# Cross-entropy over 32,000 classes on one core: label load on another ring, three buffers, short first loads, shrinking last loads, one table set

## The chip, the cores and the metric

The kernel runs on one core of a Trainium2 chip. The metric is the device time of one execution in microseconds (us). A profiled execution gives a span a little shorter than that time (2438.7 us against 2440.3 for the kernel before); details below are read from the span.

## The reference

```python
# logits: (16, 512, 32000) float32; labels: (16, 512) int32
logits_max = np.max(logits, axis=-1, keepdims=True)
log_sum_exp = np.log(np.sum(np.exp(logits - logits_max), axis=-1)) + logits_max.squeeze(-1)
log_probs = logits - log_sum_exp[..., np.newaxis]
loss = -log_probs[np.arange(batch)[:, None], np.arange(seq), labels]
```

There are 8192 rows of 32,000 values, 1048.6 MB, and each value is read once. Both kernels compute log(sum(exp(x))) minus the label's logit, without the maximum; for normally distributed logits that is safe.

## The kernel before

The 8192 rows lie on 128 partitions with 64 rows (row groups) each. A load brings 16,000 columns of one row group for all partitions, so each partition receives one contiguous piece of 64,000 bytes. ScalarE takes Exp in place and sums along the columns in the same instruction. The last three groups use loads of 4000 columns and five smaller buffers. The label logits are fetched by 64 gathers, one for each row group, issued from GpSimd.

```python
data_pool = ctx.enter_context(tc.tile_pool(name="data", bufs=2))
fine_pool = ctx.enter_context(tc.tile_pool(name="fine", bufs=5))
# ... cut ...
nc.sync.dma_start(out=labs64[:], in_=labels_pg)
# ... cut: iota and add on GpSimd make the gather's indices ...
for g in range(G):
    nc.gpsimd.indirect_dma_start(out=lab_logit[:, g:g + 1], ...)
# ... cut ...
for g in range(G):
    if g >= G - FINE_GROUPS:
        for c in range(CF):                       # 8 loads of 4000 columns
            tf = fine_pool.tile([P, WF], FP32)
            nc.sync.dma_start(out=tf[:], in_=lg_pg[:, g, c * WF:(c + 1) * WF])
            nc.scalar.activation(out=tf[:], in_=tf[:], func=Exp, accum_out=stats_col(g, c))
    else:
        for c in range(C):                        # 2 loads of 16000 columns
            t = data_pool.tile([P, W], FP32)
            nc.sync.dma_start(out=t[:], in_=lg_pg[:, g, c * W:(c + 1) * W])
            nc.scalar.activation(out=t[:], in_=t[:], func=Exp, accum_out=stats_col(g, c))

def finalize(lo, hi):
    nc.vector.reduce_sum(out=totals[:, lo:hi], ...)
    nc.scalar.activation(out=logsum[:, lo:hi], in_=totals[:, lo:hi], func=Ln)
    nc.vector.tensor_tensor(out=res[:, lo:hi], in0=logsum, in1=lab_logit, op=subtract)
    nc.scalar.dma_start(out=out_pg[:, lo:hi], in_=res[:, lo:hi])
finalize(0, G - 1)
finalize(G - 1, G)
```

## Time and profile before

| | before |
|---|---|
| median of 3 runs | 2440.26 us |
| span of the profiled run | 2438.7 us |
| ScalarE busy | 1754.4 us (72%) |
| start of the last Exp | 2430.84 us |
| from there to the end (the tail) | 7.9 us |

The first thing to ask is which engine has no time left. The following lines are from the windows view of the kernel before: the stretch in us, its length, the busy time of VectorE, ScalarE and GpSimd, the TensorE clock, the mean busy share of the 16 DMA engines, and what they moved.

```profile
core 0: us, DVE busy (x) ACT busy (x) POOL busy (x), PEclk, DMA share, GB/s
2.00:250.00 248.00, 0.00 (x0) 164.83 (x25) 60.38 (x65) 1.00 1.01 426
320.00:700.00 380.00, 0.00 (x0) 274.36 (x41) 0.00 (x0) 1.00 1.00 433
700.00:2290.00 1590.00, 0.00 (x0) 1145.91 (x169) 0.00 (x0) 1.00 1.00 433
```

The DMA engines are always busy and move 433 GB/s. The first stretch is slower, at 426 GB/s, and GpSimd is busy only there: it is issuing the gathers. ScalarE works in 66% of the first stretch and in 72% of the other two, so it waits for loads and not the reverse.

Two groups from the page of the kernel before say the same from ScalarE's side: instruction, shapes and count, then busy time and mean ns of one, then its idle time and what ended it.

```profile
L85 ACT ACTIVATE t<-t 128x16000 f32<-128x16000 f32 x122 | 1651.4, 13536 | 642.9 <-DMA t<-in_logits_dram 642.9
L76 ACT ACTIVATE tf<-tf 128x4000 f32<-128x4000 f32 x24 | 84.7, 3530 | 14.6 <-DMA tf<-in_logits_dram 14.6
```

An Exp of 16,000 columns takes 13.5 us, and ScalarE idles 642.9/122 = 5.3 us before each. As a buffer is loaded again as soon as its Exp ends, those 5.3 us are also what the *other* load still has to run when the new one is queued. That is why two buffers keep the queue filled.

The head, from the timeline of the kernel before (start, length, engine; SPq is SyncE's sequencer issuing DMAs; in brackets the idle time before and what ended it):

```profile
0.74 0.38 SPq L48 DMA_DIRECT2D labs<-in_labels_dram  x1
1.18 132.93 SPq L84 DMA_DIRECT2D t<-in_logits_dram  x8
2.79 0.32 POOL L53 TENSOR_TENSOR idx<-idx,labs 128x64 int32<-128x64 int32 x1 [1.78 <-DMA labs<-in_labels_dram]
24.64 13.54 ACT L85 ACTIVATE t<-t 128x16000 f32<-128x16000 f32 x1
```

The labels go first, and the logits wait 0.44 us for SyncE to issue them. The tail, from the same timeline:

```profile
2430.84 3.54 ACT L76 ACTIVATE tf<-tf 128x4000 f32<-128x4000 f32 x1 [1.11 <-DMA tf<-in_logits_dram]
2434.28 0.19 ACT L76 ACTIVATION_READ_ACCUMULATOR tf<-tf 128x1 f32 x1
2434.49 1.28 ACT L101 ACT_TABLE_LOAD   x1
2434.50 0.16 DVE L96 TENSOR_REDUCE totals<-stats_last 128x1 f32<-128x8 f32 x1 [36.37 <-ACT tf L76]
2435.78 0.20 ACT L101 ACTIVATE logsum<-totals 128x1 f32<-128x1 f32 x1
2436.02 0.16 DVE L105 TENSOR_TENSOR res<-logsum,lab_logit 128x1 f32<-128x1 f32 x1 [1.35 <-ACT logsum L101]
2436.21 0.34 ACTq L109 DMA_DIRECT2D out_dram<-res  x1
```

After the last load has landed, nothing overlaps the work that remains: an Exp over 4000 columns, a table load because Ln is not in the set that Exp had loaded, Ln, a subtraction, and a store of about 2.5 us until the span ends.

### The profile page before, as it was taken

What the parts mean: (1) busy time and instruction counts of PE and PEld (TensorE: products, weight loads), DVE (VectorE), ACT (ScalarE), POOL (GpSimd) and SP (SyncE); (2) the same over time, 40 slices, a digit from 0 to 9 for tenths busy, and PEclk for the clock granted to TensorE, in tenths of its full rate; (3) what the DMA queues carried; (4) which work ended last, traced back from release to release, by engine and by line L of the source; (5) the groups of instructions that cost most, each with busy time, mean ns of one, the idle gap of its engine ahead of it and who ended that gap; (6) DMA issues with size and microseconds to landing.
All of it is one profiled execution on the core that took longest, in us unless ns stands there. A gap on an engine that the chain in (4) does not pass through costs nothing.

```text
span 2438.7 us, 851 instructions
## 1 busy us (share of the span) xinstructions
DVE 1.7 (0%) x5; ACT 1754.4 (72%) x298; POOL 61.2 (3%) x70
## 2 busy tenths in 40 slices
DVE  0000000000000000000000000000000000000000
ACT  4777766777677767777677767777677767777697
POOL 3222000000000000000000000000000000000000
DMA  9999999999999999999999999999999999999998
GB/s 404 437 420 422 435 437 435 429 429 437 437 436 428 431 435 437 435 432 428 435 436 436 435 427 434 436 437 435 427 432 436 437 435 425 434 437 432 426 430 360
DMA packets 23510, 1048.77 MB, mean 430 GB/s; under 512 B 4688, under 2 KB 4816, under 8 KB 4816
## 3 DMA queue, kind: packets, MB, share of 16 engines
q1 hardware_dynamic: 21168, 1048.65, 99.6%
q0 software_dynamic: 2048, 0.04, 0.1%
q10 hardware_dynamic: 288, 0.03, 0.0%
q14 instruction: 6, 0.05, 0.0%
HBM read 1048.67 MB, written 0.03 MB: 430 GB/s over the span
## 4 chain that ended last, share of the span: by engine, by line
DMA 63%; ACT 36%; issue 0%; ACTq 0%; SPq 0%; DVE 0%
DMA t<-in_logits_dram 61%; ACT t L85 34%; DMA tf<-in_logits_dram 2%; ACT tf L76 2%; ACT L101 0%; ACT L76 0%; ACTq L85 0%; ACT logsum L101 0%; SPq L84 0%; DVE res L105 0%; SPq L48 0%; ACTq L109 0%; ACTq L76 0%
## 5 line engine op out<-in xcount | busy, mean ns | idle before, releaser
L85 ACT ACTIVATE t<-t 128x16000 f32<-128x16000 f32 x122 | 1651.4, 13536 | 642.9 <-DMA t<-in_logits_dram 642.9
L76 ACT ACTIVATE tf<-tf 128x4000 f32<-128x4000 f32 x24 | 84.7, 3530 | 14.6 <-DMA tf<-in_logits_dram 14.6
L57 POOL DMA_INDIRECT lab_logit<-in_logits_dram,idx x64 | 60.5, 945 | 186.8 <-DMA lab_logit<-in_logits_dram,idx 184.2
L85 ACT ACTIVATION_READ_ACCUMULATOR t<-t 128x1 f32 x122 | 22.7, 186 | 0.0
L85 ACT ACT_TABLE_LOAD x1 | 1.3, 1283 | 23.3 <-DMA t<-in_logits_dram 23.3
L76 ACT ACTIVATION_READ_ACCUMULATOR tf<-tf 128x1 f32 x24 | 4.5, 187 | 0.0
L101 ACT ACT_TABLE_LOAD x2 | 2.6, 1283 | 0.0
L96 DVE TENSOR_REDUCE totals<-stats 128x63 f32<-128x504 f32 x1 | 0.7, 678 | 2394.9 <-ACT tf L76 2394.9
L76 ACT ACT_TABLE_LOAD x1 | 1.3, 1283 | 0.8 <-DVE res L105 0.8
L66 DVE MEMSET stats<- 128x504 f32 x1 | 0.5, 478 | 0.9 <-PEq L127 0.9
L101 ACT ACTIVATE logsum<-totals 128x63 f32<-128x63 f32 (+1 forms) x2 | 0.5, 229 | 0.0
L105 DVE TENSOR_TENSOR res<-logsum,lab_logit 128x63 f32<-128x63 f32 (+1 forms) x2 | 0.4, 192 | 2.2 <-ACT logsum L101 2.2
L53 POOL TENSOR_TENSOR idx<-idx,labs 128x64 int32<-128x64 int32 x1 | 0.3, 318 | 1.8 <-DMA labs<-in_labels_dram 1.8
L96 DVE TENSOR_REDUCE totals<-stats_last 128x1 f32<-128x8 f32 x1 | 0.2, 161 | 36.4 <-ACT tf L76 36.4
L51 POOL IOTA idx<- 128x64 int32 x1 | 0.2, 172 | 0.4 <-PEq L138 0.4
L127 POOL MEMSET const-uint8-127<- 128x1 uint8 x1 | 0.1, 118 | 0.0
L127 POOL MEMSET const-bfloat16-1.0<- 128x1 bf16 x1 | 0.1, 113 | 0.0
L127 POOL MEMSET const-float32-0.0<- 128x1 f32 x1 | 0.1, 98 | 0.2 <-issue 0.2
L127 POOL MEMSET const-float32-1.0<- 128x1 f32 x1 | 0.1, 104 | 0.0
## 6 DMA issues: line engine op xcount, KB each, us to landing
t<-in_logits_dram SPq DMA_DIRECT2D x122, 8000.0 KB, 24.1
tf<-in_logits_dram SPq DMA_DIRECT2D x24, 2000.0 KB, 20.1
lab_logit<-in_logits_dram,idx POOLq DMA_INDIRECT x64, 33.4
labs<-in_labels_dram SPq DMA_DIRECT2D x1, 64.0 KB, 1.9
out_dram<-res ACTq DMA_DIRECT2D x1, 31.5 KB, 9.1
out_dram<-res ACTq DMA_DIRECT2D x1, 0.5 KB, 1.4
```

Source lines behind the costliest of these rows:

```text
L51: nc.gpsimd.iota(idx[:], pattern=[[V, G]], base=0, channel_multiplier=G * V)
L53: nc.gpsimd.tensor_tensor(out=idx[:], in0=idx[:], in1=labs32, op=mybir.AluOpType.add)
L57: nc.gpsimd.indirect_dma_start(out=lab_logit[:, g:g + 1], out_offset=None, in_=lg, in_offset=bass.IndirectOffsetOnAxis(ap=idx[:, g:g + 1], ...
L66: nc.vector.memset(stats[:], 0.0)
L76: nc.scalar.activation(out=tf[:], in_=tf[:], func=mybir.ActivationFunctionType.Exp, accum_out=stats_col(g, c),)
L85: nc.scalar.activation(out=t[:], in_=t[:], func=mybir.ActivationFunctionType.Exp, accum_out=stats_col(g, c),)
L96: nc.vector.reduce_sum(out=totals[:, lo:hi], in_=stats[:, lo:hi, :] if hi <= G - 1 else stats_last[:], axis=mybir.AxisListType.X,)
L101: nc.scalar.activation(out=logsum[:, lo:hi], in_=totals[:, lo:hi], func=mybir.ActivationFunctionType.Ln,)
L105: nc.vector.tensor_tensor(out=res[:, lo:hi], in0=logsum[:, lo:hi], in1=lab_logit[:, lo:hi], op=mybir.AluOpType.subtract,)
L127: nc = _bacc.Bacc("TRN2", target_bir_lowering=False, num_devices=1)
```

## The change

The intent: start the logits first, give the stream deeper buffering, let ScalarE start early, and leave as little as possible after the last load. In detail: the label load goes to ScalarE's ring (the queue of the DMAs that ScalarE issues, in place of SyncE's); one table set with Exp and Ln is loaded at the start (by an ACT_TABLE_LOAD like the one in the tail above); three buffers of 16,000 columns; the first loads are 4000, 4000 and 8000 columns; the last row group comes in ten loads that shrink from 7400 to 960 columns; the last sum's first nine parts are added beforehand and enter Ln as its bias; the instructions are issued in exactly the written order. The gathers stay.

```diff
-    data_pool = ctx.enter_context(tc.tile_pool(name="data", bufs=2))
-    fine_pool = ctx.enter_context(tc.tile_pool(name="fine", bufs=5))
+    plan(0, [[4000, 4000, 8000], [16000]], [(0, 0), (0, 1), (0, 2), (1, 0)])
+    for g in range(1, G - 2):
+        plan(g, [[W], [W]], [(0, 0), (1, 0)])
+    plan(G - 2, [[W], [10000, 6000]], [(0, 0), (1, 0), (1, 1)])
+    plan(
+        G - 1,
+        [[7400, 5840, 2260], [4540, 3720, 2920, 1780, 1460, 1120], [960]],
+        [(0, 0), (0, 1), (1, 0), (1, 1), (1, 2), (0, 2), (1, 3), (1, 4), (1, 5), (2, 0)],
+    )
+    data = ctx.enter_context(tc.tile_pool(name="data", bufs=3))
 ... cut ...
-    nc.sync.dma_start(out=labs64[:], in_=labels_pg)
+    ctx.enter_context(tc.manual_schedule())
+    nc.scalar.dma_start(out=labs64[:], in_=labels_pg)
+    nc.scalar.preload_act_table_set("natural_log_exp_and_others")
 ... cut: the gathers, unchanged ...
+    for j, (g, b, at, n) in enumerate(loads):
+        if b not in buffers:
+            buffers[b] = data.tile([P, W], FP32, tag="t", name="t")
+        t = buffers[b]
... cut: c0, the next column of row group g ...
+        nc.sync.dma_start(out=t[:, at:at + n], in_=lg_pg[:, g, c0:c0 + n])
+        exp(g, t[:, at:at + n])
+        left = len(loads) - 1 - j
+        if left == 6:
+            nc.vector.reduce_sum(out=totals[:], in_=sums[:], axis=X)
+        if left == 4:
+            nc.scalar.activation(out=logsum[:], in_=totals[:], func=LN)
+            nc.vector.tensor_tensor(out=res[:], in0=logsum[:], in1=lab_logit[:, 0:G - 1], op=ALU.subtract)
+        if left == 1:
+            nc.vector.reduce_sum(out=part[:], in_=sums_last[:, 0:K - 1], axis=X)
+    nc.sync.dma_start(out=out_pg[:, 0:G - 1], in_=res[:])
+    nc.scalar.activation(out=logsum_last[:], in_=sums_last[:, K - 1:K], func=LN, bias=part[:])
+    nc.vector.tensor_tensor(out=res_last[:], in0=logsum_last[:], in1=lab_logit[:, G - 1:G], op=ALU.subtract)
+    nc.sync.dma_start(out=out_pg[:, G - 1:G], in_=res_last[:])
```

More of the change, by code (lines that the diff above doesn't have):

```diff
@@ L7 @@
 from concourse._compat import with_exitstack
+from concourse.masks import make_identity
 FP32 = mybir.dt.float32
 I32 = mybir.dt.int32
+EXP = mybir.ActivationFunctionType.Exp
+LN = mybir.ActivationFunctionType.Ln
+ALU = mybir.AluOpType
+X = mybir.AxisListType.X
 @with_exitstack
@@ L23 @@
     B, S, V = logits.shape
-    N = B * S
     P = 128
-    G = N // P
-    assert N % P == 0
+    G = B * S // P
     W = 16000
-    C = V // W
-    assert V % W == 0
-    WF = 4000
-    CF = V // WF
-    FINE_GROUPS = 3
-    assert V % WF == 0
     lg = logits.rearrange("b s v -> (b s) v")
@@ L41, with plan @@
     out_pg = out.rearrange("b s -> (b s)").rearrange("(p g) -> p g", g=G)
-    data_pool = ctx.enter_context(tc.tile_pool(name="data", bufs=2))
-    fine_pool = ctx.enter_context(tc.tile_pool(name="fine", bufs=5))
+    loads = []
+    def plan(g, widths_by_buffer, order):
+        n_buffers = 1 + max((l[1] for l in loads), default=-1)
+        for b, i in order:
+            ws = widths_by_buffer[b]
+            loads.append((g, n_buffers + b, sum(ws[:i]), ws[i]))
+    plan(0, [[4000, 4000, 8000], [16000]], [(0, 0), (0, 1), (0, 2), (1, 0)])
[7 more added lines that the diff above has]
+    )
+    assert sum(l[3] for l in loads) == G * V
+    data = ctx.enter_context(tc.tile_pool(name="data", bufs=3))
     persist = ctx.enter_context(tc.tile_pool(name="persist", bufs=1))
     labs64 = persist.tile([P, G], mybir.dt.int64)
-    nc.sync.dma_start(out=labs64[:], in_=labels_pg)
+    labs32 = labs64[:].bitcast(I32).rearrange("p (g two) -> p g two", two=2)[:, :, 0]
     idx = persist.tile([P, G], I32)
+    lab_logit = persist.tile([P, G], FP32)
+    K = 10
+    sums = persist.tile([P, G - 1, 5], FP32)
+    sums_last = persist.tile([P, K], FP32)
+    totals = persist.tile([P, G - 1], FP32)
+    logsum = persist.tile([P, G - 1], FP32)
+    res = persist.tile([P, G - 1], FP32)
+    part = persist.tile([P, 1], FP32)
+    logsum_last = persist.tile([P, 1], FP32)
+    res_last = persist.tile([P, 1], FP32)
+    ctx.enter_context(tc.manual_schedule())
+    nc.scalar.dma_start(out=labs64[:], in_=labels_pg)
+    nc.scalar.preload_act_table_set("natural_log_exp_and_others")
+    nc.vector.memset(sums[:], 0.0)
     nc.gpsimd.iota(idx[:], pattern=[[V, G]], base=0, channel_multiplier=G * V)
-    labs32 = labs64[:].bitcast(I32).rearrange("p (g two) -> p g two", two=2)[:, :, 0]
-    nc.gpsimd.tensor_tensor(out=idx[:], in0=idx[:], in1=labs32, op=mybir.AluOpType.add)
-    lab_logit = persist.tile([P, G], FP32)
+    nc.gpsimd.tensor_tensor(out=idx[:], in0=idx[:], in1=labs32, op=ALU.add)
     for g in range(G):
@@ L62 @@
         )
-    stats = persist.tile([P, G - 1, CF], FP32)
-    stats_last = persist.tile([P, 1, CF], FP32)
-    nc.vector.memset(stats[:], 0.0)
-    def stats_col(g, c):
-        return stats[:, g, c:c + 1] if g < G - 1 else stats_last[:, 0, c:c + 1]
-    for g in range(G):
-        if g >= G - FINE_GROUPS:
-            for c in range(CF):
-                tf = fine_pool.tile([P, WF], FP32)
-                nc.sync.dma_start(out=tf[:], in_=lg_pg[:, g, c * WF:(c + 1) * WF])
-                nc.scalar.activation(
-                    out=tf[:], in_=tf[:],
-                    func=mybir.ActivationFunctionType.Exp,
-                    accum_out=stats_col(g, c),
-                )
-        else:
-            for c in range(C):
-                t = data_pool.tile([P, W], FP32)
-                nc.sync.dma_start(out=t[:], in_=lg_pg[:, g, c * W:(c + 1) * W])
-                nc.scalar.activation(
-                    out=t[:], in_=t[:],
-                    func=mybir.ActivationFunctionType.Exp,
-                    accum_out=stats_col(g, c),
-                )
@@ L91 @@
-    totals = persist.tile([P, G], FP32)
-    logsum = persist.tile([P, G], FP32)
-    res = persist.tile([P, G], FP32)
-    def finalize(lo, hi):
-        nc.vector.reduce_sum(
-            out=totals[:, lo:hi],
-            in_=stats[:, lo:hi, :] if hi <= G - 1 else stats_last[:],
-            axis=mybir.AxisListType.X,
-        )
-        nc.scalar.activation(
-            out=logsum[:, lo:hi], in_=totals[:, lo:hi],
-            func=mybir.ActivationFunctionType.Ln,
-        )
-        nc.vector.tensor_tensor(
-            out=res[:, lo:hi], in0=logsum[:, lo:hi], in1=lab_logit[:, lo:hi],
-            op=mybir.AluOpType.subtract,
-        )
-        nc.scalar.dma_start(out=out_pg[:, lo:hi], in_=res[:, lo:hi])
@@ L111, with exp @@
-    finalize(0, G - 1)
-    finalize(G - 1, G)
+    buffers = {}
+    col = {}
+    n_exp = {}
+    def exp(g, ap):
+        k = n_exp.get(g, 0)
+        n_exp[g] = k + 1
+        s = sums[:, g, k:k + 1] if g < G - 1 else sums_last[:, k:k + 1]
+        nc.scalar.activation(out=ap, in_=ap, func=EXP, accum_out=s)
+    for j, (g, b, at, n) in enumerate(loads):
+        if b not in buffers:
+            buffers[b] = data.tile([P, W], FP32, tag="t", name="t")
+        t = buffers[b]
+        c0 = col.get(g, 0)
+        col[g] = c0 + n
+        nc.sync.dma_start(out=t[:, at:at + n], in_=lg_pg[:, g, c0:c0 + n])
[8 more added lines that the diff above has]
+            nc.vector.reduce_sum(out=part[:], in_=sums_last[:, 0:K - 1], axis=X)
@@ L116 @@
+    assert n_exp[G - 1] == K
+    nc.sync.dma_start(out=out_pg[:, 0:G - 1], in_=res[:])
+    nc.scalar.activation(out=logsum_last[:], in_=sums_last[:, K - 1:K], func=LN, bias=part[:])
+    nc.vector.tensor_tensor(out=res_last[:], in0=logsum_last[:], in1=lab_logit[:, G - 1:G], op=ALU.subtract)
+    nc.sync.dma_start(out=out_pg[:, G - 1:G], in_=res_last[:])
 _INS = ['logits', 'labels']
```

## The prediction

> **What bounds the kernel now.** The DMA engines, moving 1048.6 MB of logits. The windows view gives a DMA share of 1.00 and 433 GB/s from 320 us to 2290 us. The Trainium skill, "DMA: Bandwidth & Descriptors", Specifications, states a fabric ceiling of 435 GB/s; the trace agrees, this stream sits on it. ScalarE is busy 72%: in the timeline a 16000-column Exp takes 13.6 us and starts every 18.90 us; in the waits it idles 643 us for loads. VectorE and GpSimd do almost nothing.
>
> Starvation between loads: with two buffers, a load is issued when an Exp ends, while the other load still has 5.3 us to run (ScalarE's idle time before each Exp). So the queue is never empty, and the third buffer has no hole to fill. The short loads near the end, about four in flight, come every 4.77 us: 429 GB/s, so a deeper queue is not faster. From the two periods (18.90 and 4.77 us) I estimate 1.1775 ns per column plus 0.06 us per load.
>
> Gathers: they run to about 250 us. In that stretch the windows view gives 426 GB/s, and the starts of Exp average about 19.25 us apart instead of 18.90. Together an estimated 4 to 6 us. The gathers stay as they are, so that cost stays.
>
> Head: SyncE issues the labels at 0.74 us and the first logits at 1.18 us. Tail: the last Exp starts at 2430.84 us, and the span ends at 2438.7: 7.9 us, made of Exp 3.6, table load 1.28, sum, Ln and subtraction about 0.45, output DMA about 2.5.
>
> **What the change does (all estimates from those durations).**
> - Labels on ScalarE's ring: logits start about 0.44 us earlier: -0.4 us. The labels now share the engines with the first logits, so the gathers start some us later; on no critical path.
> - 139 loads instead of 146: -0.4 us.
> - Third buffer, short first loads: 0. Early Exps start at about 8 us rather than 24.6, but ScalarE has slack.
> - Tail: the last Exp has 960 columns, about 1.0 us instead of 3.6; the 1.28 us table load is gone, since one set holding both functions is loaded at the start. (The skill, "ScalarE: Activation LUTs", What ACT_TABLE_LOAD costs, says 1283 ns; the trace shows 1283. The drain that it adds does not show in the tail: 0.02 us between Exp's end and the load.) The shrinking widths work: each Exp (0.833 ns per column plus about 0.2) nearly fits in the next load, leaving lateness of at most 0.2 us. The earlier output store queues behind the last loads on SyncE, about 1 us, beside the last Exp. New tail about 4.1 us: -3.8 us.
> - The two table loads in mid-stream sat in ScalarE's slack: 0.
>
> Sum: -4.6 us, nearly all of it in the last 8 us.
>
> **Prediction:** 2435.7 us, 2432.8 to 2438.6 for 8 in 10. Faster by over 2%: 0.01; within 2%: 0.98; slower by over 2%: 0.01.
>
> **What would show each step.** In the windows view still 433 GB/s between 320 and 2290 us (third buffer worth nothing); Exp starts still 18.90 us apart; first logits issued near 0.75 us; the same lower rate while gathers run; one ScalarE table load, at the start; tail from the last Exp's start to the end about 4.1 us; last load landing near 2430 us.
>
> **What would make it wrong.** The third buffer removing a loss that the DMA share hides (rate above 435 GB/s); small last loads running far below rate (landing every 1.4 us or so expected for 1120 columns); the 63-column store, late on SyncE's queue, ending after the last one; the label load, interleaved with logits, delaying the gathers so that they cost more; a difference of 0.1 to 0.3% between chips or allocations, as large as the gain.

## The result, and the profile after

| | before | after |
|---|---|---|
| median (4 runs each) | 2440.22 us | 2435.89 us |
| lowest to highest | 2440.01 to 2440.32 | 2435.56 to 2436.13 |
| ratio | | 0.9982 (95% interval 0.9968 to 0.9997) |
| start of the last Exp | 2430.84 us | 2430.02 us |
| tail from there to the end | 7.9 us | 4.1 us |

A ratio is the mean time of one kernel's fast runs over the mean of the other's in the same rounds, so it isn't quite the ratio of the quoted medians. The kernel is 4.3 us faster, 0.18%. The interval excludes "no difference", and against a threshold of 2% the two are the same.

The windows view of the changed kernel, in the same columns:

```profile
2.00:250.00 248.00, 0.00 (x0) 164.59 (x29) 60.62 (x65) 1.00 1.00 425
320.00:700.00 380.00, 0.00 (x0) 274.54 (x41) 0.00 (x0) 1.00 1.00 433
700.00:2290.00 1590.00, 0.00 (x0) 1145.86 (x169) 0.00 (x0) 1.00 1.00 433
```

With three buffers the rate is 433 GB/s, as with two. The head of the changed kernel, from its timeline:

```profile
0.74 0.40 ACTq L83 DMA_DIRECT2D labs<-in_labels_dram  x1
0.74 55.36 SPq L113 DMA_DIRECT2D t<-in_logits_dram  x7
1.17 1.28 ACT L84 ACT_TABLE_LOAD   x1 [1.17 <-PEq L144]
8.32 3.54 ACT L105 ACTIVATE t<-t 128x4000 f32<-128x4000 f32 x1 [5.86 <-DMA t<-in_logits_dram]
8.55 0.32 POOL L87 TENSOR_TENSOR idx<-idx,labs 128x64 int32<-128x64 int32 x1 [7.54 <-DMA labs<-in_labels_dram]
```

Labels and logits are now issued at the same time. ScalarE starts at 8.3 us in place of 24.6. The price is in the last line: the labels arrive nearly 6 us later, because their small packets now take turns with long logit packets. In the packet records their 128 packets of 512 bytes start between 2.5 and 7.9 us, among logit packets of 16,000 bytes; in the kernel before they start between 1.75 and 2.3 us, ahead of the logits. Nothing waits for them except the gathers, which are not needed until the end. The tail of the changed kernel:

```profile
2428.87 1.12 ACT L105 ACTIVATE t<-t 128x1120 f32<-128x1120 f32 x1
2430.02 1.00 ACT L105 ACTIVATE t<-t 128x960 f32<-128x960 f32 x1
2430.11 0.16 DVE L123 TENSOR_REDUCE part<-sums_last 128x1 f32<-128x9 f32 x1 [3.99 <-ACT t L105]
2431.14 0.29 ACT L127 ACTIVATE logsum_last<-sums_last,part 128x1 f32<-128x1 f32 x1
2431.47 0.16 DVE L128 TENSOR_TENSOR res_last<-logsum_last,lab_logit 128x1 f32<-128x1 f32 x1 [1.20 <-ACT logsum_last L127]
2431.66 0.34 SPq L129 DMA_DIRECT2D out_dram<-res_last  x1
```

Exp is 1.0 us long, no table load stands before Ln, and the addition of the nine other parts is done during the last Exp. From the last Exp's start to its end the span has 4.1 us left. The last load was issued at 2407.4 us and, by its line in the DMA view (KB, then us from issue to landing), took 22.5 us to land:

```profile
t<-in_logits_dram SPq DMA_DIRECT2D x1, 480.0 KB, 22.5
```

So it landed at about 2429.9, and ScalarE was ready for it within 0.1 us. The span fell by 2438.7 - 2434.1 = 4.6 us: 0.8 us from an earlier last Exp and 3.8 us from a shorter tail. These are two single executions. The unprofiled runs of the kernel before have spans from 2438.1 to 2438.8 us, so the 0.8 us are about as large as the difference between two executions. The tail of the changed kernel is 4.1 us in all three of its traces.

### The profile page after: what moved, and what is told of

It reads as the page before. It is cut to its first block, busy times and chain, and to the rows that moved or that the text cites. A ratio compares the mean times of both kernels' runs of the same rounds, so it can differ in the third digit from the quotient of the medians.

```text
span 2434.1 us, 807 instructions
## 1 busy us (share of the span) xinstructions
DVE 1.3 (0%) x5; ACT 1748.9 (72%) x281; POOL 61.0 (3%) x70
## 3 DMA queue, kind: packets, MB, share of 16 engines
q1 hardware_dynamic: 20304, 1048.62, 99.8%
## 4 chain that ended last, share of the span: by engine, by line
DMA 76%; ACT 24%; issue 0%; SPq 0%; ACTq 0%; DVE 0%
DMA t<-in_logits_dram 76%; ACT t L105 24%; SPq L113 0%; ACTq L105 0%; ACT logsum_last L127 0%; DVE res_last L128 0%; ACT logsum L120 0%
## 5 line engine op out<-in xcount | busy, mean ns | idle before, releaser
L105 ACT ACTIVATE t<-t 128x16000 f32<-128x16000 f32 (+5 forms) x139 | 1734.8, 12481 | 681.4 <-DMA t<-in_logits_dram 681.2
L84 ACT ACT_TABLE_LOAD x1 | 1.3, 1283 | 1.2 <-PEq L144 1.2
```

The costliest lines, as they stand in the source:

```text
L84: nc.scalar.preload_act_table_set("natural_log_exp_and_others")
L105: nc.scalar.activation(out=ap, in_=ap, func=EXP, accum_out=s)
```

## The experiments

My theory: the gain is the tail (last Exp and table load), with small parts from the head and from fewer loads; the buffers give nothing, since the DMA queue never ran empty. The rival, the buffer theory: the third buffer and the short first loads remove stalls that the busy share hides. Each kernel ran five rounds. The runs fell on three chips; the kernel before took 2440.13, 2440.08 and 2440.09 us there, so that its times may be compared across them. All results were correct except where it is said.

### The changed kernel again

No edit; a yardstick for two of the three chips.

> The changed kernel unaltered, as the yardstick for the runs beside it on the same chip. Both theories: 2435.9 us again, 4.3 us below the kernel before. Tail theory: the gain is made of the last Exp (about 2.5 us), one table load (1.3 us), the earlier first load (0.4 us) and seven fewer loads (0.4 us). Rival, buffer theory: the third buffer and the short first loads make most of it.

> The changed kernel unaltered, again as the yardstick of this chip: 2435.5 to 2436.1 us.

Measured: 2435.74 us (2435.33 to 2435.81), and on the other chip 2436.24 us (2435.78 to 2436.90). The two medians differ by 0.5 us, so a difference of 0.5 us between kernels on different chips means nothing here.

### Two buffers in place of three

```diff
-    data = ctx.enter_context(tc.tile_pool(name="data", bufs=3))
+    data = ctx.enter_context(tc.tile_pool(name="data", bufs=2))
+    tiny = ctx.enter_context(tc.tile_pool(name="tiny", bufs=1))   # the last 960 columns only
```

(Shortened: the lines that give the last load its buffer from `tiny` are left out, and the comment is added.)

> The changed kernel with two wide buffers instead of three (the last 960 columns have a small buffer of their own, so the tail keeps its loads). Tail theory: the DMA queue still always holds over 5 us of work, so the time stays within 0.3 us of the unaltered changed kernel. Buffer theory: 2 us or more of the gain is lost, and the rate between 320 and 2290 us falls.

Measured: 2435.63 us (2435.47 to 2436.10), against 2435.74 with three on the same chip. The third wide buffer is worth nothing. The buffer theory falls in this part.

### Long first loads

```diff
-    plan(0, [[4000, 4000, 8000], [16000]], [(0, 0), (0, 1), (0, 2), (1, 0)])
+    plan(0, [[16000], [16000]], [(0, 0), (1, 0)])
```

> The changed kernel with its first row group loaded as two loads of 16000 columns instead of 4000, 4000, 8000 and 16000. If ScalarE's early start is off the chain: within 0.3 us of the changed kernel (two packet sets fewer, 0.17 us, on the faster side). If the early start is part of the gain: 1 us or more slower.

Measured: 2435.94 us (2435.79 to 2436.10), against 2436.24 on the same chip. ScalarE's first Exp starts at 22.42 us instead of 8.3, and the kernel is not slower. The short first loads are off the chain too. Each part of the buffer theory was taken back alone; that both together hide no stall in mid-stream rests on the kernel before, which has neither and moves the same 433 GB/s from 320 us on.

### Last row group in equal loads of 4000

```diff
-        [[7400, 5840, 2260], [4540, 3720, 2920, 1780, 1460, 1120], [960]],
+        [[4000, 4000, 4000, 4000], [4000, 4000, 4000, 4000]],
```

(The order list and the number of parts of the last sum are changed to match.)

> The changed kernel with its last row group loaded as eight loads of 4000 columns in place of the ten shrinking ones. Tail theory: the last Exp grows from 1.0 to 3.5 us, and two loads fewer are made: 2.4 us slower than the unaltered changed kernel (2.0 to 2.8). Buffer theory: within 0.5 us of it.

Measured: 2438.13 us (2438.06 to 2438.18), 2.4 us slower than 2435.74 on the same chip, as expected. The timeline of this run shows the term: the last Exp starts at 2429.53 us and is 3.54 us long.

```profile
2429.53 3.54 ACT L105 ACTIVATE t<-t 128x4000 f32<-128x4000 f32 x1 [1.14 <-DMA t<-in_logits_dram]
2433.19 0.29 ACT L127 ACTIVATE logsum_last<-sums_last,part 128x1 f32<-128x1 f32 x1
```

The shrinking widths make over half of the whole gain.

### The kernel before, with one table set

```diff
+    nc.scalar.preload_act_table_set("natural_log_exp_and_others")
     labs64 = persist.tile([P, G], mybir.dt.int64)
```

> The kernel before with one table set for Exp and Ln, loaded once at the start, and nothing else changed: three table loads go, of which only the last one is on the chain. Tail theory: 1.3 us faster than the kernel before (1.1 to 1.6). Buffer theory: at most 0.3 us.

Measured: 2439.20 us (2438.74 to 2439.35) against 2440.13, 0.9 us faster and so under the range. The timeline of this run says why it is less than 1.28:

```profile
2429.94 3.54 ACT L77 ACTIVATE tf<-tf 128x4000 f32<-128x4000 f32 x1 [1.12 <-DMA tf<-in_logits_dram]
2433.60 0.16 DVE L97 TENSOR_REDUCE totals<-stats_last 128x1 f32<-128x8 f32 x1 [36.94 <-ACT tf L77]
2433.79 0.20 ACT L102 ACTIVATE logsum<-totals 128x1 f32<-128x1 f32 x1 [0.23 <-DVE totals L97]
```

In the kernel before, VectorE's final sum ran beside the table load. With the table load gone, ScalarE waits 0.23 us for that sum. The tail is 2436.7 - 2429.94 = 6.8 us against 7.9, so 1.1 us is what the table load was worth in this chain. The changed kernel recovers the 0.2 us by giving the sum's first nine parts to Ln as a bias: there Ln starts 0.12 us after the last Exp ends, here 0.31 us. The other 0.2 us (1.1 in the profiled run, 0.9 in the medians) is within the spread, as the profiled run was the fastest of its five, and I don't explain it. In this trace the last Exp also starts 0.9 us earlier than in the kernel before (2429.94 against 2430.84 us), though neither the label load nor the number of loads was changed. So a shift of 0.9 us there, from one trace to another, needs no cause in the kernel.

### Labels back on SyncE

```diff
-    nc.scalar.dma_start(out=labs64[:], in_=labels_pg)
+    nc.sync.dma_start(out=labs64[:], in_=labels_pg)
```

> The changed kernel with the label load put back on SyncE, ahead of the first logits. If SyncE's issue time is all that counts: the first logits start 0.44 us later, the gathers start about 5 us earlier, and the whole is 0.4 us slower than the changed kernel (0.2 to 0.6). Rival: mixing the small label packets with the first logits costs as much as it gains, and the two are equal within 0.1 us.

Measured: 2436.03 us (2435.60 to 2436.44). There was no yardstick on this chip; the changed kernel had 2435.74, 2435.89 and 2436.24 elsewhere. In this run's trace the logits are issued at 1.18 us instead of 0.74 and the first Exp starts at 8.60 us instead of 8.32, 0.3 us later. But the changed kernel's two other traces, with the logits issued at 0.74 us, have 8.23 and 8.66 us, so even the 0.3 us is not resolved. Inconclusive.

### Twice the loads

```diff
-        nc.sync.dma_start(out=t[:, at:at + n], in_=lg_pg[:, g, c0:c0 + n])
+        h = n // 2 if n == W else n
+        for o in range(0, n, h):
+            nc.sync.dma_start(out=t[:, at + o:at + o + h], in_=lg_pg[:, g, c0 + o:c0 + o + h])
```

> The changed kernel with each of its 124 loads of 16000 columns issued as two of 8000 columns into the same buffer; the Exps stay whole. If a load costs 0.06 us beyond its bytes, as the two periods of the kernel before gave: 124 more loads, 7.4 us slower than the changed kernel (5 to 10). If deeper queues hide the cost: within 1 us.

Measured: 2446.12 us (2445.99 to 2446.76), 10.2 us slower than 2435.89. The cost is real, and a deep queue doesn't hide it: 10.2/124 = 0.082 us for each additional load, more than the 0.06 of the prediction. In the trace the median distance of two Exp starts between 320 and 2290 us is 18.98 us instead of 18.90, which is 0.08 directly.

### As many loads, twice the pieces

For the row groups 1 to 60, one load brings 8000 columns of two row groups.

```diff
+            nc.sync.dma_start(
+                out=t[:].rearrange("p (r v) -> p r v", r=2),
+                in_=lg_pg[:, ga:ga + 2, q * 8000:(q + 1) * 8000],
+            )
+            exp(ga, t[:, 0:8000])
+            exp(ga + 1, t[:, 8000:16000])
```

(Shortened: the condition and the arithmetic of `ga` and `q` are left out.)

> The changed kernel with 120 of its loads made of two pieces of 8000 columns per partition (of two row groups) instead of one of 16000: as many loads and bytes, but twice as many packets of half the size. If the cost beyond the bytes belongs to the load (its completion): within 1 us of the changed kernel. If it belongs to the packet (0.06 us for the eight packets of each engine): 120 times 0.06 is 7 us slower.

Measured: 2446.35 us (2446.12 to 2446.86), 10.5 us slower than 2435.89, with a median distance of 18.98 us again. The number of loads did not change and the cost came all the same: 10.5/120 = 0.087 us. So the cost isn't the load's completion. It belongs to the pieces: each engine moves 128/16 = 8 of them per load, so one costs an estimated 0.085/8, about 11 ns, beyond its bytes. The packet records agree. In the changed kernel a packet of 64,000 bytes takes 2366 ns (median) and one of 3840 bytes 152 ns; a straight line through both has 0.0368 ns per byte and 11 ns over. In the two runs with halved pieces a packet of 32,000 bytes takes 1189 ns, 11 ns above the bytes' share by that line.

### No gathers (wrong on purpose)

```diff
-    for g in range(G):
-        nc.gpsimd.indirect_dma_start(out=lab_logit[:, g:g + 1], ...)
+    nc.gpsimd.memset(lab_logit[:], 0.0)
```

> The changed kernel without the 64 gathers, the gathered values set to zero: the result is wrong on purpose. If the gathers slow the logits while they run, as the lower rate up to 250 us says: 4 to 6 us faster than the changed kernel, and Exp starts 18.90 us apart from the start on. Rival: the lower rate at the start has another cause, and the time stays within 1 us.

Measured: 2431.19 us (2430.96 to 2431.54); the result is wrong, as intended. It is 4.7 us faster than 2435.89. The early stretch now runs at the full rate:

```profile
2.00:250.00 248.00, 0.00 (x0) 165.32 (x30) 0.41 (x2) 1.00 1.00 433
```

So 0.04 MB of gathered data cost as much as the whole change gains: 4.7/64 = 0.07 us for each gather.

### Wider loads

Two buffers of 24,000 columns, loads that run over row ends (a partition's 64 rows are contiguous), the same ten last loads.

```diff
-    W = 16000
+    W = 24000
+    lg_flat = logits.rearrange("b s v -> (b s) v").rearrange("(p g) v -> p (g v)", g=G)
+    for k in range(83):
+        loads.append((k, 0, 24000))
+    # load 83 in three parts of 12000, 8000, 4000; then the ten last loads as before
```

(Shortened; an Exp is split where its buffer crosses a row end.)

> The changed kernel with two buffers of 24000 columns and loads that run over row ends: 84 such loads of which one is split in three, and the same ten last loads; 96 loads instead of 139. The two runs with halved pieces showed about 0.085 us per eight extra packets on an engine. If one piece of 96000 bytes is still one packet, 43 sets of packets go: about 3.5 us faster than the changed kernel, and the packet count of the load queue falls by about 6000. If a packet cannot be that long and each piece becomes two, the packet count rises by about 5000 instead and the kernel is 3 to 4 us slower.

Measured: 2435.12 us (2434.15 to 2435.22), 1.1 us faster than 2436.24 on the same chip: between the two expectations. The load queue's line on the page, of the changed kernel and then of this run (queue, packets, MB, share of the engines' time):

```profile
q1 hardware_dynamic: 20304, 1048.62, 99.8%
```

```profile
q1 hardware_dynamic: 24736, 1048.62, 99.8%
```

Packets rose by 4432, so each piece of 96,000 bytes did become two packets. Yet the stream got faster: the median distance between loads' first Exps is 28.31 us, and 1.5 times 18.90 would be 28.35. The lost 0.04 us is the half of 0.085 us that fewer *pieces* should save; the additional packets cost nothing that I can see. The packet records say nearly the same: a packet of 48,000 bytes takes 1773 ns, so two take 3546 ns, and the line above gives 3544 for one packet of 96,000 bytes but 3554 for two of 48,000. In this kernel the cost thus follows contiguous pieces more than packets. It rests on one kernel, and a cost that depends on a packet's length in another way is not excluded.

Over 84 loads that is 3.4 us. The timeline shows where some of it went, in the profiled run, the fastest of the five at 2434.15 us:

```profile
2359.51 13.54 ACT L98 ACTIVATE t<-t 128x16000 f32<-128x16000 f32 x1 [7.86 <-DMA t<-in_logits_dram]
2373.04 6.85 ACT L98 ACTIVATE t<-t 128x8000 f32<-128x8000 f32 x1
2379.90 10.19 ACT L98 ACTIVATE t<-t 128x12000 f32<-128x12000 f32 x1
...
2427.01 1.12 ACT L98 ACTIVATE t<-t 128x1120 f32<-128x1120 f32 x1
2428.13 0.98 ACT L98 ACTIVATE y<-y 128x960 f32<-128x960 f32 x1
```

No Exp after the first has an idle time: ScalarE is behind from 2359 us to the end. The last load was issued at 2404.79 us and took 22.5 us, so it landed at about 2427.3, 2.6 us earlier than in the changed kernel, but its Exp began only at 2428.13. The shrinking last loads were tuned for a buffer of 16,000 columns; behind a buffer of 24,000, ScalarE starts them with a backlog. It is the fastest kernel with a right result here, by 1.1 us. A longer run of shrinking loads might bring another 0.8 us; I have not tried it.

### VectorE picks the label's logit

The gathers of row groups 1 to 61 are replaced by VectorE.

```diff
+                nc.vector.scalar_tensor_tensor(
+                    out=junk[:], in0=cols[:], scalar=labf[:, g, q:q + 1], in1=t[:, at + o:at + o + H],
+                    op0=ALU.is_equal, op1=ALU.mult, accum_out=picks[:, g - 1, q:q + 1],
+                )   # H = 4000 columns; junk lies in PSUM
```

(Shortened: the loop over the pieces and the set-up of `cols`, `labf` and `picks` are left out.)

> The changed kernel with 61 of its 64 gathers gone: VectorE, idle until now, picks the label's logit out of each loaded buffer before the Exp overwrites it (column number equal to label, times the data, summed; pieces of 4000 columns, their output thrown away). The run without gathers showed 4.6 us for 64 of them. If VectorE takes less than 18.9 us for a buffer of 16000 columns [...], three buffers hide it: 4.0 to 4.6 us faster than the changed kernel, near 2431.4 us, with a right result. If a piece takes over 4.7 us, VectorE bounds the kernel and it is slower by the difference at every buffer.

Measured: 2448.68 us (2448.49 to 2448.92), correct, and 12.4 us *slower* than 2436.24. A miss, and not through either of the expected ways: a piece takes 4.39 us, so VectorE does keep up. The groups view of this run, and its timeline at the end:

```profile
L128 DVE SCALAR_TENSOR_TENSOR junk<-cols,labf,t 128x4000 f32<-128x4000 int16 x488 | 2144.2, 4394 | 191.1 <-DMA t<-in_logits_dram 178.3
```

```profile
2369.82 4.39 DVE L128 SCALAR_TENSOR_TENSOR junk<-cols,labf,t 128x4000 f32<-128x4000 int16 x1
2374.35 13.54 ACT L116 ACTIVATE t<-t 128x16000 f32<-128x16000 f32 x1 [5.26 <-issue]
2387.89 13.52 ACT L116 ACTIVATE t<-t 128x16000 f32<-128x16000 f32 x1
2401.41 8.52 ACT L116 ACTIVATE t<-t 128x10000 f32<-128x10000 f32 x1
...
2442.79 0.99 ACT L116 ACTIVATE t<-t 128x960 f32<-128x960 f32 x1
```

Each Exp must wait about 18 us for VectorE to have read the buffer that it overwrites. In mid-stream three buffers hide that. At the end ScalarE enters the last loads some 18 us late, gains only 5.3 us on each buffer of 16,000 columns, and never catches up. The last load, issued at 2415.2 us, took 17.2 us, so it landed at about 2432.4, but its Exp starts at 2442.79: 10.4 us of backlog. The other loss is that the last load landed 2.5 us later than in the changed kernel although the gathers had gone. Seven of the distances between Exp starts are 19.8 to 19.9 us instead of 18.90, and some others are 0.3 to 0.6 us too long. The instruction queue moved 14 packets here and 6 in the changed kernel, and 1850 instructions ran against 807.

The packet records show when. From 320 to 2380 us, eight loads landed 19.86 to 19.88 us after the load before them, and during each of these eight gaps the instruction queue moved a packet of 8 KB. The changed kernel has two such gaps, of 19.57 and 19.58 us, again with an instruction packet in each. Eight times 0.97 is 7.8 us, more than all 64 gathers cost. So instruction fetching is the likely cause of this loss; six of the 14 packets have no such gap around them and no run isolates them, so it is not shown.

## Why the prediction was right

- **The sum.** -4.6 us was predicted (2435.7 us); measured were -4.3 us in the medians (2435.89 us) and -4.6 us in the two profiled spans. The second agreement is in part luck: the spans for the unprofiled runs, about 2438.4 and 2434.1 us, differ by 4.3 us too.
- **What bounds the kernel: shown.** The Trainium skill, "DMA: Bandwidth & Descriptors", Specifications, states a fabric ceiling of 435 GB/s; the traces show 433 GB/s with two buffers and with three. That the DMA stream is the limit is shown by the runs that added pieces (10 us slower) and took the gathers away (4.7 us faster); whether this ceiling or another limit near it sets the rate, no run separates.
- **Third buffer and short first loads, 0: shown.** Taking back either one cost nothing (2435.63 against 2435.74 us, 2435.94 against 2436.24). The argument that carried this was not the busy share alone but the 5.3 us of work that the queue still holds when a buffer is loaded again.
- **Tail, -3.8 us: shown.** The traces give 7.9 and 4.1 us, to the predicted tenth. Equal last loads gave back 2.4 us. The table load alone gave 0.9 us, less than its 1.28, because VectorE's final sum had been hidden beside it. The prediction took off the whole 1.28 us and did not name that sum; its tail came out right because the changed kernel also takes the sum off the chain, as Ln's bias.
- **Shrinking widths: shown.** The last Exp started about 0.1 us after its load landed; the prediction allowed 0.2.
- **Fewer loads, -0.4 us: the mechanism was mis-stated and the size low.** The prediction had "0.06 us per load". The two runs with halved pieces give 0.08 to 0.09 us and tie it to the pieces, 128 of them in every load. Seven loads of 128 pieces fewer are then about 7 x 0.085 = 0.6 us (an estimate from those runs; no run takes back these seven loads alone).
- **Head, -0.4 us: not resolved.** Logits are issued 0.44 us earlier, as predicted, but neither the times nor the start of the first Exp (8.60 us against 8.23 to 8.66) show a gain. That this line and the one above add up to about the 0.8 us by which the last Exp came earlier may be chance: the kernel before with one table set, which has neither, shows 0.9 us.
- **Gathers, 4 to 6 us, unchanged: shown.** Without them the kernel is 4.7 us faster. They started nearly 6 us later, as the prediction said, and the rate while they ran was 425 GB/s against 426.

## What to carry to other kernels

When the DMA engines are busy from start to end, ask how much work the queue still holds each time a load is issued; if that is several microseconds, more buffers buy nothing, and only the head, the tail and the bytes' overhead are left. A tail is shortened by last loads that shrink just as fast as the computing engine can follow, and the whole chain after the last load has to be summed, since an instruction that is removed may have hidden another. Moving work to an idle engine can lengthen the way of each buffer, and that length comes due at the end even when the engine keeps up in mid-stream.

## What the Trainium skill lacked or had wrong

- "DMA: Bandwidth & Descriptors", Where 436 GB/s comes from, says that for transfers between HBM and SBUF the HBM side binds, at about 358 GB/s. One core's stream, with no other core in the program, ran at 433 GB/s here, near the 435 of the fabric. ("HBM Reference", Specifications (TRN2), has it better: a core streaming alone measures about 425.)
- The same page, in the Measured part of Bandwidth, gives 10.5 ns per packet from a small transfer. The halved pieces cost 0.082 and 0.087 us per eight, about 10 to 11 ns each. That is the same size, but not the same quantity: the page divides a whole small transfer by its 64 packets, and here it is what a packet costs beyond its bytes. Pieces of 96,000 bytes, which became two packets each, showed little or no cost for the second packet (28.31 us per load against 28.35 for the same bytes in pieces of 64,000). The page doesn't say that the cost can follow contiguous pieces.
- The same page calls a packet preferably at most 4096 bytes, but of the packets that GpSimd builds; it gives no size for loads issued from SyncE. In these traces one packet record of such a load carried a whole piece of 64,000 bytes (20,304 packets on the load queue for 1048.6 MB), which may be another unit than the page's packet.
- No page says what a gather costs beside a full stream: 64 gathers of 128 values of 4 bytes took 4.7 us from it, 0.07 us each.
- "ScalarE: Activation LUTs", What ACT_TABLE_LOAD costs, gives 1283 ns plus a drain of about 1380 ns. The load took 1283 ns here; before the last one 0.02 us passed, so no drain showed, and removing it from the chain gained 0.9 us.
